# Spreading a second lane of work over a matmul stage, and re-dealing the buffers the two share

## The chip, the cores and the metric

The kernel runs on one core of one Trainium2 chip. The metric is the device time of one execution in microseconds; three runs gave 1947.91, 1949.51 and 1950.28 us, and the median, 1949.51 us, is the time before. One more execution was profiled; its numbers are in the section on the profile.

## The reference, cut to what matters

The model is one layer of a hybrid backbone on 256 latent and 256 context tokens of width 2048, all in float32. Its last part is an expert lookup ("PEER"): each token picks 8 x 16 = 128 of 16384 experts, and each expert has a row of 2048 numbers in a table u and one in a table v.

```python
def block(args):
    xb, eb, gb = args                       # tokens, their experts, their gates
    a = jnp.einsum('nd,nhkd->nhk', xb, jnp.take(u_tab, eb, axis=0))
    w = (gb * jax.nn.gelu(a.astype(jnp.float32))).astype(xb.dtype)
    return jnp.einsum('nhk,nhkd->nd', w, jnp.take(v_tab, eb, axis=0))
```

So per token there are 128 dot products with gathered u rows, a gelu, and a weighted sum of 128 gathered v rows. Each table has 16384 x 2048 x 4 bytes, 134 MB.

## The kernel before, in words

Everything up to row 0 of the u stage (projections, the mLSTM, the output projection, the queries) is not touched. The expert lookup splits the tokens in two groups.

- **The 192 dense tokens** (NA). For them TensorE multiplies the whole u table: 128 "rows" of the table (1 MB each, a transfer `...<-in_u_t` issued by SP), each in two halves. ScalarE makes `hi`, VectorE `lo` of each half (three buffers of each), and TensorE runs 16 pairs of matmuls `ups<-hf,hi` and `ups<-hf,lo` per row; ScalarE and VectorE then put the result in row i2 of the table W (`ut<-ups`, `W<-ut,ups`). This is the u stage. After it, `one_hots` and `pick` choose each token's 128 numbers out of W, four tokens at a time, and give weights `wA`; then one gather per token brings its 128 v rows (1 MB, `...<-in_v_rows`, issued by GpSimd, POOL in the profile) and eight matmuls `y<-...,wA` (`add_rows`) sum them. That is the y stage, 192 gathers long.
- **The 64 gathered tokens** are never multiplied with the whole table. For them a lane of work runs beside the u stage (`gen_gather`): 128 steps, each with a 1 MB gather. 64 are "u" steps (a gather of u rows, and on VectorE a dot product `...<-...,hB` of 2048 elements), 64 are "v" steps (a gather of v rows, eight matmuls into `adaps` or `yb`, and before each a small selector `wB` on ScalarE). The v steps follow the u steps by eight (`SUB`).

The kernel is written down in one pass by Python, with no scheduler behind it: instructions stand on each engine in the order in which the program issues them. The order comes from a planner's clock, `clock["t"]`, that each matmul moves on by an assumed duration. A lane is a generator that yields how long it wants to wait on that clock; after each half row `pump` advances the lanes that are due. In the lane of the gathered tokens each step ends with `yield GP`, 4.65 us of that clock; a lane that is behind may catch up by at most LAG, 3 us. What the lane hasn't done when the last row has been issued is issued by `drain()`, between the first `pick` and the y stage.

The gathers take their buffers from a list, `gaths`: `gath0`, `gath1` (and from row 66 `gath2`), and "lent" ones. W has 192 x 128 numbers per partition, 12 pieces of 8 KB; piece i is not written before row i*2048/192, so until then it can be lent. Pieces 1, 2, 3, 5, 7 and 9 are lent to the u table's transfers (`LENT_U`), 4, 6, 8 and, from row 66, 11 to gathers (`LENT`), and 10 from row 66 to u. Beside lent pieces, u has `rawA`, `rawB` and from row 66 `raw0`. `no_extra` ends the lending of a piece six rows ahead of its row; `lent_back` advances the lane, two rows ahead, until the piece is free. When the last row is out, `rawA`, `rawB`, `raw0` and `hB` become gather buffers too, so that the y stage rotates seven: the three `gath` and these four.

`gather` takes the first free buffer or returns False; `fetch` issues as many gathers of the list `to_get` as there are buffers. At the middle of the second half of the v steps the 192 dense gathers are put behind the others in `to_get`.

In the lines below L354 is the one place that issues a matmul, L133 the one that issues ScalarE and VectorE work, L268 the u table's transfer, L1367 the gather; so work is told apart by its tiles.

Of the kernel before, what the change touches and what calls it, by code (L numbers as in the profile page):

```python
# [34 lines left out]
KD = D // P  # L35
# [5 lines left out]
NK = 128  # L41
# [3 lines left out]
NA = T - NB  # L45
BT = 32
REP = P // BT
STEPS = PH * TOPK // REP
# [30 lines left out]
UTB = 3  # L79
RT_AT = 66  # L80
RT_DELAY = 60.0
GP = 4.65
NAF = 2
GY = 8.0
GATES_AT = 7
# [93 lines left out]
def build(tc, a, stack, dbg=None):  # L179
    nc = tc.nc  # L180
    ten, pool, sync = nc.tensor, nc.gpsimd, nc.sync
    clock = dict(t=0.0)
# [3 lines left out]
    def open_pool(name, side="left", **kw):  # L186
        cm = tc.tile_pool(name=name, bufs=1, side=side, reuse_waits="tile", **kw)
        return cm, cm.__enter__()

    def close_pool(p):  # L190
        p[0].__exit__(None, None, None)
# [10 lines left out]
    def mm_ps(name="mm"):  # L202
        return psp.tile([P, 512], F32, name=name, tag="mm", bufs=4)
# [30 lines left out]
    wides = Slots(lambda u: u.wide.used or u.wide.lo is not None, 2048)  # L234
# [101 lines left out]
    def drain(only=None):  # L336
        def left():
            return [k for k, q in lanes.items() if q and (only is None or k in only)]
        while left():
            for k in left():  # L340
                advance(k)
# [39 lines left out]
    def rstd_of(out, ss, n):  # L381
        vec.tensor_scalar(out, ss, 1.0 / n, EPS, op0=OP.mult, op1=OP.add)
        act.activation(out, out, AF.Sqrt)
        vec.reciprocal(out, out)
# [645 lines left out]
    R = {}  # L1030
    gaths = Slots(lambda u: u.used, 2048)

    LENT_U = (1, 2, 3, 5, 7, 9)
    LENT = (4, 6, 8, 11)
    x1d = tc.dram_tile([P, KD, T], F32, name="x1_spill")

    def make_hf(u):
        drain(only=("ada",))
        x1 = Y["x"]
        ss = mm_ps("ss1")  # L1040
        mm(ss[:, 0:T], ones, Y["sq"], start=True, stop=False)
        mm(ss[:, 0:T], ones, Y["last"], start=False, stop=True)
        prepare()
        rs = con.tile([P, T], F32, name="rs1", tag="rs1")
        rstd_of(rs, ss[:, 0:T], D)
        araws.drop(V["B"])
        close_pool(V["pb"])
        R["rh"] = open_pool("rh", side="right")
        R["rsb"] = open_pool("rsb", side="right")
        R["rs"] = open_pool("rs", side="right")  # L1050
        H, S, SB = R["rh"][1], R["rs"][1], R["rsb"][1]
        hf = H.tile([P, KD, 2, T], F32R, name="hf", tag="hf")
        hB = H.tile([P, D], F32, name="hB", tag="hB")
        R.update(hB=hB, hf=hf, hfs=hf.rearrange("p k s t -> p s k t"))
        R["keys"] = S.tile([P, 2, NK], F32, name="keys")
        sync.dma_start(R["keys"], a["keys"])
        sync.dma_start(x1d, x1)
        dump("x1", x1)
        n2 = 2 * PH * TOPK
        R["val"] = SB.tile([P, 2, n2], F32, name="val")  # L1060
        R["ix"] = SB.tile([P, 2, n2], U32, name="ix")
        R["sc"] = SB.tile([P, PH, TOPK], F32, name="sc")
        R["ci"] = SB.tile([P, PH, TOPK], U32, name="ci")
        R["e12"] = SB.tile([P, 3, PH, TOPK], F32, name="e12")
        R["h64"] = S.tile([P, KD, NB], F32, name="h64")
        shift, hm = mod[:, 3, 0], {}

        def scaled(k):
            hm[k] = S.tile([P, T], F32, name="hm1", tag="hm1", bufs=4)
            vec.scalar_tensor_tensor(hm[k], x1[:, k], gm[:, 2, k:k + 1], rs, op0=OP.mult, op1=OP.mult)  # L1070

        skew(KD, scaled,
             lambda k: act.activation(hf[:, k, 0], hm[k], AF.Identity, bias=shift[:, k:k + 1]),
             lambda k: vec.scalar_tensor_tensor(hf[:, k, 1], hm[k], shift[:, k:k + 1],
                                                hf[:, k, 0].bitcast(F32), op0=OP.add, op1=OP.subtract))
        spawn("hA", copy_hB())

        close_pool(pa)
        R["w"] = open_pool("w")
        R["W"] = R["w"][1].tile([P, NK, NA], F32, name="W")  # L1080
        flat = R["W"].rearrange("p e n -> p (e n)")
        room = [flat[:, c * 2048:(c + 1) * 2048] for c in range(NK * NA // 2048)]
        R["room"], R["scr"] = room, room[11]
        R["s0"] = room[10].rearrange("p (h k) -> p h k", k=NK)
        for i in LENT_U:
            wides.place(("row", i), room[i], i * 2048 // NA - 3)
        for i in LENT[:-1]:
            gaths.place(("lent", i), room[i])

    hBd = tc.dram_tile([P, D], F32, name="hB_spill")  # L1090

# [203 lines left out]
    def open_w(u):  # L1295
        drain(only=("hA", "score", "look"))
        close_pool(R["rs"])
        R["t"] = open_pool("wt")
        R["gp"] = open_pool("gp")
        gaths.add(R["gp"][1], "gath", F32, 2)  # L1300
        spawn("score", gen_route(1, RP1))
        spawn("score", gen_wait(RT_DELAY))
        spawn("score", gen_top(0, RP0))
        spawn("score", gen_route(0, RP0))

    def gen_wait(us):
        yield us
# [14 lines left out]
    def open_px(u):  # L1322

        drain(only=("score",))
        iT = R["iT"]
        vec.scalar_tensor_tensor(R["eA"], iT[:, 0, 0:NA], float(NK), iT[:, 1, 0:NA], op0=OP.mult, op1=OP.add)
        close_pool(R["rsb"])
        R["px"] = open_pool("px", side="right")
        wides.add(R["px"][1], "raw", F32, 1)
        gaths.add(R["px"][1], "gath", F32, 1)  # L1330

        wides.place(("row", 10), R["room"][10], 10 * 2048 // NA - 3)
        gaths.place(("lent", 11), R["room"][11])

    for i, tag in enumerate(("rawA", "rawB")):
        wides.take_over(pipe, tag, lambda i=i: all(s[3] is None or raws.done(s[3]) for s in raws.slots[2 * i:2 * i + 2]))
# [22 lines left out]

    got = collections.deque()  # L1360

    def gather(tab, idx):
        g = Unit(None, False, None)
        g.raw = gaths.take(g)
        if g.raw is None:
            return False
        pool.indirect_dma_start(out=g.raw, out_offset=None, in_=tab,  # L1367
                                in_offset=bass.IndirectOffsetOnAxis(ap=idx, axis=0))
        got.append(g)
        return True  # L1370

    to_get = collections.deque()
# [14 lines left out]
    def gen_gather():  # L1387

        aB, n = R["aB"], STEPS
        ops = []  # L1390
        for b in range(2):
            for s in range(n):
                ops += [("u", b, s)] + [("v", b, s - SUB)] * (s >= SUB)
                if s % SUB == SUB - 1:
                    ops.append(("fin", b, s + 1 - SUB))
            ops += [("v", b, s) for s in range(n - SUB, n)]

        ops.insert(ops.index(("v", 0, n - SUB)) + 2, ("hB", 1, 0))
        for kind, b, s in ops:
            if kind in ("u", "v"):  # L1400
                to_get.append((a[kind + "_rows"], R["idx"][:, b, s:s + 1]))
        scaled = {}

        def scale(b, s):
            w = scaled[b, s] = R["t"][1].tile([P, BT], F32, name="wB", tag="wB", bufs=2)
            act.activation(w, selb, AF.Copy, scale=aB[:, b, s:s + 1])

        fetch()
        yield 4.0
        for j, (kind, b, s) in enumerate(ops):  # L1410
            if kind == "v" and b == 1 and s == n // 2:
                to_get.extend((a["v_rows"], R["eA"][:, t:t + 1]) for t in range(NA))
            if kind == "fin":
                while "gates" not in R:
                    yield 1.0
                some = slice(s, s + SUB)
                act.activation(aB[:, b, some], aB[:, b, some], GELU)
                vec.tensor_tensor(aB[:, b, some], aB[:, b, some], R["gB"][:, b, some], op=OP.mult)
                if s == 0:
                    YB[b] = ada_ps() if b == 0 else sm_ps("yb")  # L1420
                yield 2.0
                scale(b, s)
                yield 0.0
                continue
            if kind == "hB":
                R["hB"] = R["rh"][1].tile([P, D], F32, name="hB", tag="hB")
                sync.dma_start(R["hB"], hBd)
                continue
            fetch()
            g = got.popleft()  # L1430
            if kind == "u":
                vec.scalar_tensor_tensor(g.raw, g.raw, 1.0, R["hB"], op0=OP.mult, op1=OP.mult,
                                         accum_out=aB[:, b, s:s + 1])
                g.used = True
            else:
                add_rows(YB[b], scaled.pop((b, s)), g, s == 0, s == n - 1)
                if (s + 1) % SUB:
                    scale(b, s + 1)
            fetch()
            yield GP  # L1440

    for i2 in range(NK):
        for i in LENT:
            row = i * 2048 // NA
# [308 lines left out]
```

## Time and profile before

| of the profiled execution | |
|---|---|
| its time | 1945.05 us |
| its span, first to last instruction | 1943.3 us |
| median of three runs without the profiler | 1949.51 us |
| PE busy / DVE / ACT / POOL, share of the span | 88% / 63% / 36% / 20% |
| moved by DMA | 670.20 MB, mean 345 GB/s |
| u stage: first and last `ups` matmul | 750.0 and 1424.8 us |
| y stage: first and last `y` matmul | 1448.7 and 1932.2 us |

PE is TensorE, PEld its weight loads, DVE VectorE, ACT ScalarE, POOL GpSimd, SP the engine that issues plain transfers. A busy share is an average over stages with different limits: PE is busy for 299.67 of the 300 us from 800 to 1100, and for 335.88 of the 480 us from 1440 to 1920. "Share" of DMA is the mean busy share of the 16 DMA engines. A wait is put down to what ended it. Program lines of the kernel after are four to five higher than those of the kernel before.

### The profile page before, as it was taken

The numbers are of one execution on the slowest core, as the hardware profiler recorded it, in microseconds if no ns is written. First come the engines' busy times: TensorE is split into PE (matmuls) and PEld (weight loads), VectorE is DVE, ScalarE is ACT, GpSimd is POOL, SyncE is SP. The second block draws the span as 40 slices with busy tenths as digits, with TensorE's granted clock in tenths as the row PEclk, the third lists the DMA queues.
The fourth block names the chain that finished last, engine by engine and source line by source line (L and its number), as shares of the span: only waits on it lengthen the run. The fifth ranks groups of instructions, "written<-read, shape, count | busy, mean of one in ns | idle before, by whom it ended". The sixth has DMA issues, their size and how long they took to land.

```text
span 1943.3 us, 29970 instructions
## 1 busy us (share of the span) xinstructions
PE 1713.3 (88%) x11882; PEld 1354.1 (70%) x11882; DVE 1226.5 (63%) x2498; ACT 702.1 (36%) x1105; POOL 384.2 (20%) x324
## 2 busy tenths in 40 slices
PE   4999999999899999899999999999976767667775
PEld 2689789979799899898988799889842222222221
DVE  5346868776698669889998587777633323323232
ACT  4235325555544544454444445444411100101000
POOL 0000000000000000332223232333333343333331
PEclk8999999999999899999999999999989888998888
DMA  9975878776688754999999999999989999999996
GB/s 396 393 266 178 291 239 303 274 249 213 212 321 308 274 185 147 390 413 371 390 384 407 395 403 417 378 389 400 389 349 420 420 421 421 421 420 421 421 421 287
DMA packets 115869, 670.20 MB, mean 345 GB/s; under 512 B 12688, under 2 KB 15248, under 8 KB 53264
## 3 DMA queue, kind: packets, MB, share of 16 engines
q1 hardware_dynamic: 69648, 332.72, 46.0%
q0 software_dynamic: 46080, 335.56, 42.2%
q8 instruction: 93, 1.52, 0.3%
q14 instruction: 48, 0.39, 0.1%
HBM read 662.99 MB, written 5.24 MB: 344 GB/s over the span
## 4 chain that ended last, share of the span: by engine, by line
PE 68%; DMA 23%; DVE 4%; issue 3%; ACT 1%; POOL 0%; SPq 0%; POOLq 0%; ACTq 0%; DVEq 0%
PE ups L354 29%; PE mm L354 25%; DMA gath<-in_v_rows,iT 8%; DMA hB<-in_v_rows,iT 5%; DMA raw<-in_v_rows,iT 3%; PE adaps L354 3%; PE y L354 2%; DMA rawB<-in_v_rows,iT 2%; DMA ring<-in_ada 2%; DMA rawA<-in_v_rows,iT 2%; PE pick L354 1%; PE num L354 1%; PE yb L354 1%; PE sm L354 1%; PE pc L354 1%
## 5 line engine op out<-in xcount | busy, mean ns | idle before, releaser
L354 PE MATMUL ups<-hf,hi 128*128 128x384 f32 x2048 | 601.5, 366 | 0.0
L354 PE MATMUL ups<-hf,lo 128*128 128x192 f32 x2048 | 515.6, 252 | 8.7 <-DVE lo L133 8.4
L354 PEld LDWEIGHTS ups<-hf,hi 128*128 128x128 f32 x2048 | 386.9, 189 | 48.5 <-issue 42.8
L354 PEld LDWEIGHTS ups<-hf,lo 128*128 128x128 f32 x2048 | 393.6, 192 | 12.2 <-DVE lo L133 12.2
L133 DVE SCALAR_TENSOR_TENSOR oh<-c,iT,pick 128x128 f32<-128x128 f32 x192 | 55.4, 345 | 305.4 <-PE pick L354 305.4
L133 DVE TENSOR_TENSOR lo<-rawA,hi 128x1024 fp32r<-128x1024 f32 x134 | 163.7, 1223 | 103.7 <-ACT hi L133 95.4
L133 DVE TENSOR_TENSOR lo<-rawB,hi 128x1024 fp32r<-128x1024 f32 x132 | 161.3, 1222 | 92.3 <-ACT hi L133 88.4
L1367 POOL DMA_INDIRECT W<-in_u_rows,iT x24 | 37.7, 1570 | 847.0 <-DMA W<-in_u_t 778.4
L133 ACT ACTIVATE hi<-rawA 128x1024 fp32r<-128x1024 f32 x134 | 141.6, 1057 | 147.8 <-PE ups L354 73.8
L1367 POOL DMA_INDIRECT gath<-in_v_rows,iT x119 | 135.1, 1136 | 270.6 <-PE y L354 119.0
L133 ACT ACTIVATE hi<-rawB 128x1024 fp32r<-128x1024 f32 x132 | 139.4, 1057 | 130.3 <-PE ups L354 64.6
L354 PE MATMUL mm<-xL,hi 128*128 128x256 f32 x864 | 181.1, 290 | 4.8 <-ACT xL L133 1.7
L133 ACT ACTIVATE hi<-W 128x1024 fp32r<-128x1024 f32 x114 | 120.8, 1060 | 149.7 <-PE ups L354 146.7
L133 DVE TENSOR_TENSOR lo<-W,hi 128x1024 fp32r<-128x1024 f32 x114 | 138.7, 1221 | 42.5 <-ACT hi L133 37.4
L354 PEld LDWEIGHTS mm<-xL,hi 128*128 128x128 f32 x864 | 144.0, 192 | 14.2 <-issue 7.5
L354 PE MATMUL y<-gath,wA 128*32 128x512 f32 x664 | 96.7, 660 | 64.2 <-DMA gath<-in_v_rows,iT 61.5
L133 DVE SCALAR_TENSOR_TENSOR adacc<-araw,early,adacc 128x1024 f32<-128x1024 f32 x120 | 152.4, 1278 | 0.0
L133 ACT ACTIVATE uA<-uA 128x4 f32<-128x4 f32 x48 | 9.9, 205 | 383.9 <-DVE oh L133 383.9
L354 PE MATMUL mm<-xL,lo 128*128 128x256 f32 x432 | 122.4, 283 | 0.0
L354 PEld LDWEIGHTS pick<-W,oh 128*128 128x128 f32 x384 | 77.8, 241 | 55.5 <-issue 52.7
L354 PE MATMUL mm<-hf,hi 128*128 128x256 f32 x512 | 98.7, 292 | 6.1 <-ACT hf L133 5.3
L354 PEld LDWEIGHTS y<-gath,wA 128*32 128x32 f32 x664 | 13.8, 111 | 121.0 <-DMA gath<-in_v_rows,iT 107.9
(284 smaller groups left out, 3021.6 us busy)
## 6 DMA issues: line engine op xcount, KB each, us to landing
araw<-in_ada SPq DMA_DIRECT2D x128, 512.0 KB
W<-in_u_t SPq DMA_DIRECT2D x57, 1024.0 KB
ring<-in_ada SPq DMA_DIRECT2D x32, 1024.0 KB
rawB<-in_u_t SPq DMA_DIRECT2D x28, 1024.0 KB
rawA<-in_u_t SPq DMA_DIRECT2D x28, 1024.0 KB
raw<-in_u_t SPq DMA_DIRECT2D x15, 1024.0 KB
rawB<-in_wout SPq DMA_DIRECT2D x16, 512.0 KB
rawA<-in_wout SPq DMA_DIRECT2D x16, 512.0 KB
```

The source lines that it names most:

```text
L133: return f(*args, **kw)
L354: ten.matmul(out, lhsT, rhs, start=start, stop=stop, skip_group_check=True, **kw)
L1367: pool.indirect_dma_start(out=g.raw, out_offset=None, in_=tab, in_offset=bass.IndirectOffsetOnAxis(ap=idx, axis=0))
```

## The change

The lane's wait is no longer a constant. When the u stage opens, the program works out when it will end on the planner's clock (`u_end`, 0.97 of the assumed matmul time of 128 rows and 64 v steps), and each step waits for the time that is left, divided by the steps that are left. Piece 9 goes from u to the gathers, and piece 10 too: u keeps five lent pieces (1, 2, 3, 5, 7), gathers have six (4, 6, 8, 9, then 10 and 11 from row 66). Dense gathers carry a row number that keeps them out of lent pieces.

```diff
-GP = 4.65
+LANE = 0.97
...
-    LENT_U = (1, 2, 3, 5, 7, 9)
-    LENT = (4, 6, 8, 11)
+    LENT_U = (1, 2, 3, 5, 7)
+    LENT = (4, 6, 8, 9, 10, 11)
...
-        for i in LENT[:-1]:
-            gaths.place(("lent", i), room[i])
+        for i in LENT[:-2]:
+            gaths.place(("lent", i), room[i], NK)
...
     def open_w(u):
...
+        R["u_end"] = clock["t"] + LANE * (NK * KD * (2 * NA / 2400.0 + 0.107) + 2 * STEPS * 4 * 0.244)
...
-        wides.place(("row", 10), R["room"][10], 10 * 2048 // NA - 3)
-        gaths.place(("lent", 11), R["room"][11])
+        for i in LENT[-2:]:
+            gaths.place(("lent", i), R["room"][i], NK)
...
-    def gather(tab, idx):
+    def gather(tab, idx, dense=False):
         g = Unit(None, False, None)
+
+        g.row = NK + 1 if dense else 0
...
-                to_get.extend((a["v_rows"], R["eA"][:, t:t + 1]) for t in range(NA))
+                to_get.extend((a["v_rows"], R["eA"][:, t:t + 1], True) for t in range(NA))
...
-            yield GP
+
+            yield max(0.5, (R["u_end"] - clock["t"]) / (len(ops) - j))
```

The instructions are the same in kind and number; their places and buffers differ. Counted in the programs' order, at the start of a row of the u stage, these steps of the lane have been issued, these gathers, and these rows of the u table:

| row | steps before, now | gathers before, now | u transfers before, now |
|---|---|---|---|
| 8 | 3, 3 | 8, 9 | 16, 15 |
| 66 | 60, 68 | 63, 72 | 73, 71 |
| 96 | 89, 100 | 93, 105 | 101, 100 |
| 122 | 116, 127 | 119, 130 | 126, 126 |

On ScalarE (ACT) at the end of the u stage: `ut` closes a row, `hi` is half a row of the u table, `wB` is the selector of a v step, `uA` and `ysb` belong to the y stage. Before:

```order
L133 ACTIVATE ut<-ups 128x192
L133 ACTIVATE hi_13974<-rawA 128x1024
L133 ACTIVATE iT<-iT 128x8
L133 ACTIVATE ut<-ups 128x192
L133 ACTIVATE wB<-c_68,iT 128x32 x3
L133 ACTIVATE ut<-ups 128x192
L133 ACTIVATE uA<-uA 128x4
L133 ACTIVATE wB<-c_68,iT 128x32 x5
```

And now:

```order
L133 ACTIVATE ut<-ups 128x192
L133 ACTIVATE hi_13997<-rawA 128x1024
L133 ACTIVATE hi_14017<-raw_13911 128x1024
L133 ACTIVATE ut<-ups 128x192
L133 ACTIVATE hi_14041<-raw_13911 128x1024
L133 ACTIVATE ut<-ups 128x192 x2
L133 ACTIVATE uA<-uA 128x4 x2
L133 ACTIVATE ysb<-adaps 128x512
```

Eight selectors stood here, three before the last row is closed and five behind it; now there is none, and the last v step stands at row 122.

On TensorE (PE) right behind the last `ups` matmul and the one-hots (`i`): `pick` reads W for four tokens, `yb` is a v step, `y` a dense token. Before:

```order
L354 MATMUL pick<-W,oh 128x128 x4
L354 MATMUL yb<-gath_13948,wB 32x512 x4
L354 MATMUL yb<-gath_14024,wB 32x512 x4
L354 MATMUL yb<-gath_14048,wB 32x512 x4
L354 MATMUL yb<-rawA,wB 32x512 x4
L354 MATMUL yb<-rawB,wB 32x512 x4
L354 MATMUL yb<-raw_14090,wB 32x512 x4
L354 MATMUL pick<-W,oh 128x128 x4
```

And now, from the pick on (two picks stand together, as x8, then four pairs of the one-hots of the third batch, of which the last is shown):

```order
L354 LDWEIGHTS ib
L354 MATMUL i_14158<-ib 128x128
L354 MATMUL y<-gath_13775,wA 32x512 x4
L354 MATMUL y<-gath_13807,wA 32x512 x4
L1592 MATMUL yT<-c_68,ysb 128x128 x4
L354 MATMUL y<-gath_13859,wA 32x512 x4
L354 MATMUL y<-rawA,wA 32x512 x4
L354 MATMUL ss_14203<-z,ones 128x32
```

Six v steps stood between the first pick and the first `y`; now none does, and the first three dense tokens lie in `gath` buffers, which were gathered into before the end of the u stage.

On SP, the u table's transfers a little behind row 66, in the buffers' names. Before:

```order
L268 DMA raw_11143<-in_u_t 128x2048
L268 DMA W<-in_u_t 128x2048 x2
L268 DMA rawB<-in_u_t 128x2048
L268 DMA rawA<-in_u_t 128x2048
L268 DMA raw_11384<-in_u_t 128x2048
```

And now:

```order
L268 DMA W<-in_u_t 128x2048
L268 DMA raw_10938<-in_u_t 128x2048
L268 DMA rawB<-in_u_t 128x2048
L268 DMA rawA<-in_u_t 128x2048
L268 DMA raw_11113<-in_u_t 128x2048
```

Before, u rotated five buffers here (two of them lent, W), down to three from its transfer 102 on; now it has `rawB`, `rawA` and `raw` alone from transfer 70 on.

## Rows read from the trace of the kernel before

**Rows 1.** Stages: busy us (instructions) per engine, granted clock, DMA share, GB/s.

```profile
core 0: us, PE busy (x) PEld busy (x) DVE busy (x) ACT busy (x) POOL busy (x), PEclk, DMA share, GB/s
800.00:860.00 60.00, 60.00 (x420) 56.99 (x420) 52.61 (x59) 31.56 (x44) 19.89 (x12) 1.00 1.01 420
800.00:1100.00 300.00, 299.67 (x2078) 270.12 (x2078) 264.28 (x497) 143.57 (x208) 87.36 (x56) 1.00 0.98 394
1100.00:1400.00 300.00, 297.39 (x2052) 270.24 (x2051) 220.34 (x243) 143.66 (x206) 94.36 (x57) 0.99 0.99 397
1412.00:1432.00 20.00, 18.62 (x131) 13.23 (x130) 8.56 (x24) 4.69 (x13) 8.24 (x8) 1.00 0.70 245
1440.00:1920.00 480.00, 335.88 (x2122) 129.87 (x2122) 153.27 (x706) 38.23 (x84) 178.36 (x189) 0.88 1.01 421
```

**Rows 2.** Waits on ScalarE in the u stage, 800 to 1425: us, times, longest.

```profile
ACT hi L133 <- PE ups L354: 296.3, 219, 3.3
...
ACT hi L133 <- DMA rawB<-in_u_t: 2.6, 1, 2.6
```

**Rows 3.** The chain that ended last: start us, us, what.

```profile
1125.06 50.62 PE ups L354 x352
...
1383.48 9.34 PE ups L354 x64
1393.82 9.34 PE ups L354 x64
...
1915.69 15.52 DMA gath<-in_v_rows,iT
```

**Rows 4.** The tile ups: ns min/median/max, first and last start.

```profile
L354 PE MATMUL ups<-hf,lo x2048: 249/250/529, 750.3 to 1424.8; 128*128 128x192 f32 x187
```

**Rows 5.** TensorE in order of time, 1418 to 1462: start us, us, tiles [idle before].

```profile
1424.94 1.07 PE L354 MATMUL yb<-gath,wB 128*32 128x512 f32 x8
...
1429.11 1.06 PE L354 MATMUL yb<-gath,wB 128*32 128x512 f32 x8
...
1438.05 1.93 PE L354 MATMUL yb<-gath,wB 128*32 128x512 f32 x8 [6.10 <-DMA gath<-in_v_rows,iT]
...
1445.52 1.07 PE L354 MATMUL yb<-raw,wB 128*32 128x512 f32 x8 [0.79 <-DMA raw<-in_v_rows,iT]
...
1448.67 1.06 PE L354 MATMUL y<-hB,wA 128*32 128x512 f32 x8
```

**Rows 6.** GpSimd, gathers: the lane's first, and around the end of the u stage.

```profile
778.81 2.11 POOL L1367 DMA_INDIRECT W<-in_u_rows,iT  x1 [778.36 <-DMA W<-in_u_t]
...
1414.81 1.78 POOL L1367 DMA_INDIRECT gath<-in_v_rows,iT  x1 [1.75 <-PE yb L354]
1422.85 0.94 POOL L1367 DMA_INDIRECT gath<-in_v_rows,iT  x1 [6.27 <-PE yb L354]
...
1431.29 0.94 POOL L1367 DMA_INDIRECT hB<-in_v_rows,iT  x1 [0.30 <-issue]
...
1450.04 0.94 POOL L1367 DMA_INDIRECT hB<-in_v_rows,iT  x1 [2.22 <-PE y L354]
```

**Rows 7.** VectorE: the lane's first dot product, and the first weights wA.

```profile
787.31 2.29 DVE L133 SCALAR_TENSOR_TENSOR W<-W,hB 128x2048 f32<-128x2048 f32 x1 [3.42 <-DMA W<-in_u_rows,iT]
...
1430.85 0.68 DVE L133 TENSOR_SCALAR wA<-c,uA 128x32 f32<-128x32 f32 x4
```

**Rows 8.** Two stretches of 2 us, columns as in Rows 1.

```profile
1422.00:1424.00 2.00, 2.00 (x19) 1.52 (x11) 0.00 (x0) 0.32 (x1) 0.94 (x1) 1.00 0.03 8
1424.00:1426.00 2.00, 2.00 (x17) 1.00 (x16) 0.35 (x1) 0.33 (x1) 0.00 (x0) 1.00 0.71 180
```

**Rows 9.** DMA queues, 800 to 860: packets, MB, share of 16 engines.

```profile
q0 software_dynamic: 1739, 12.67, 51.0%
q1 hardware_dynamic: 1709, 12.45, 49.9%
```

**Rows 10.** Page, costliest groups: ScalarE's hi and VectorE's lo, mean ns.

```profile
L133 DVE TENSOR_TENSOR lo<-rawA,hi 128x1024 fp32r<-128x1024 f32 x134 | 163.7, 1223 | 103.7 <-ACT hi L133 95.4
...
L133 ACT ACTIVATE hi<-rawA 128x1024 fp32r<-128x1024 f32 x134 | 141.6, 1057 | 147.8 <-PE ups L354 73.8
```

## The prediction

> **What bounds the kernel now.** I read the stages first [rows 1]. In the u stage two things are nearly full at once: TensorE is busy for 299.67 of 300 us and 297.39 of 300 us, and the DMA engines show a share of 0.98 and 0.99. Busy alone doesn't say which of the two holds, so next come the waits. ScalarE's `hi` waits 296.3 us for TensorE to give a buffer back and, the longest of its transfer waits, 2.6 us for one from DRAM [rows 2]. Data is there before TensorE wants it: TensorE bounds the u stage, DMA only keeps step. From 1440 to 1920 it is the other way round: DMA share 1.01 at 421 GB/s, TensorE busy for 70% [rows 1]. The last gather is issued at 1915.69 and has landed 15.52 us later, at 1931.2, and the chain runs through it [rows 3]; the rest of the span, 12.1 us, is the last tokens' end.
>
> Between the two stages DMA runs dry: from 1412 to 1432 it moves 245 GB/s [rows 1], so 20 x (1 - 245/421) = 8.4 us of its time are lost. The reason stands in the rows of TensorE and GpSimd: the last `ups` matmul starts at 1424.8 [rows 4], but seven v steps come behind it, from 1424.94 to 1446.6 [rows 5], and their gathers are issued one by one as buffers come free, 1414.81, 1422.85 and on [rows 6]. The first gather for a dense token goes out only at 1431.29 (into hB) and is used at 1448.67 [rows 5, 6]. So the y stage, which is a pure stream of 192 gathers, starts its stream late. Its pace: first landing 1448.67, last 1931.2, 191 gathers between, 482.5/191 = 2.526 us each [rows 3, 5].
>
> **The change part by part.**
>
> *The seven v steps move into the u stage.* There they cost TensorE time, since TensorE is the bound. Without v steps 352 `ups` take 50.62 us, 0.1438 us each, and 64 of them (two rows) 9.20 us; with one v step the same two rows repeat after 1393.82 - 1383.48 = 10.34 us [rows 3]. A v step costs 1.14 us. 57 are inside the u stage now, 64 will be: 7 x 1.14 = 8.0 us, so it would end at 1424.8 + 8.0 = 1432.8, if nothing else in it moves.
>
> *More gathers in the first half.* By row 66 the lane has issued 72 gathers instead of 63, and u 71 transfers instead of 73: 7 MiB more (each is 1 MiB) in the stretch that is 800 to 1100 now. There DMA moved 394 GB/s x 300 us = 118.2 MB, 112.7 MiB [rows 1]; it will be 119.7. With both queues full it moved 420 GB/s from 800 to 860 [rows 1], 2.497 us per MiB, so this needs 299 us; TensorE will take 300 + 4 v steps x 1.14 = 304.6 us. It fits at 98%, and the gathers have a cushion: four to six are issued ahead, at 4.7 us a step (304.6 us for the 65 steps from row 8 to 66) some 19 us or more, where one alone took 8.5 us beside u transfers (issued 778.81, used 787.31) [rows 6, 7]. At 98% some land late all the same, and a late one holds VectorE or TensorE, whose queues run in order: behind a waiting dot product stand the `lo` that TensorE needs next. The least is nothing; the most, with DMA at 394 GB/s, is 119.7 x 1.0486/0.394 - 304.6 = 14 us. I take 3 us, near the lower end, since the 420 was measured with the same two streams. VectorE itself has room: 264.28 of 300 us now [rows 1], plus four dot products of 2.29 us [rows 7], 273 of 305. In the second half there is less to add (rows 66 to 122: 58 gathers instead of 56, 55 u transfers instead of 53), and I put nothing there. So the u stage ends at X = 1432.8 + 3 = 1435.8.
>
> *The buffers.* Pieces 9 and 10 taken from u shorten its lead; price nothing as long as three buffers do, which is a rival below. For the gathers they make the cushion just used. The dense gathers, kept out of lent pieces, get gath0 to gath2 before the end: three, which land under the last rows, as the v steps end at row 122. Then rawA, rawB, raw and hB as u gives them back, about at rows 125 to 127; those four land by about X + 2, since only 2 u transfers run beside them.
>
> *The start of the y stage.* TensorE now goes from the first pick straight on. Its first weights `wA` are ready at 1430.85 + 0.68 = 1431.5 [rows 7], 6.7 us behind the last `ups`; that chain (one-hots, pick, VectorE, gelu) is unchanged, so the first `y` runs at X + 6.7 and ends 1.06 us later [rows 5]. Seven gathers are in, 128 to 134 counted over all 320; number 135 reuses the first buffer. Now hB was issued at 1450.04, 0.3 us behind the end of the `y` that freed it (1448.67 + 1.06) [rows 5, 6], so 135 is issued at X + 8.1. DMA has been dry for some 5 us by then; the 2 MiB that SP fetches for the residual fill that hole, which they don't today. From issue to landing on an idle DMA no row shows it: below is the bare transfer of 2.5 us, above the 8.5 us of the shared one. Nearest is the issue at 1422.85, behind which DMA goes from 8 GB/s to 180 between 1424 and 1426 [rows 6, 8]: about 1.6 us to the first bytes, and 2.5 us for the rest, 4.1 us. I take that. (The Trainium skill, "DMA: Bandwidth & Descriptors", on the anatomy of one DMA of the gpsimd path, gives 2.0 us plus the bytes at 436 GB/s, so 4.4 us here as an estimate, and the sum would be 0.3 us later.) So 135 lands at X + 12.2 and DMA is full from there, as TensorE is busy for only 0.70 of the time that DMA takes for a token [rows 1].
>
> *The sum.* Number 319, the last, is 184 gathers later: X + 12.2 + 184 x 2.526 = X + 477.0 = 1912.8, against 1931.2: 18.4 us less. With the same end the profiled execution would go from 1945.05 to 1926.7 us. The three runs have their median 4.5 us above the profiled one; the difference carried over, 1949.51 - 18.4 = 1931 us.
>
> **The rivals.**
>
> *DMA in the u stage does no more than it does now.* If 394 and 397 GB/s are the mixture's ceiling and not the demand, the first half takes 14 us longer than TensorE; the second, 300 x 397 = 119.1 MB today plus 4 MiB, takes 123.3/0.397 = 311 against some 302, 9 us more. Together 23 in the place of my 3: X is 20 us later and the gain of 18 is gone, 1951 us, no change. For it speaks the share of 0.98 already, against it 420 GB/s with q0 and q1 at 51.0% and 49.9% and TensorE 60.00 of 60 us busy [rows 1, 9].
>
> *Three buffers starve u; this ends slower.* From transfer 70 on u has three. A buffer is taken up again every three rows, 15.5 us (a row is 10.34/2 = 5.17 us [rows 3]); behind the landing a `hi` of 1.06 us and two `lo` of 1.22 us take 3.5 us of that [rows 10], so a transfer may need 12.0 us, and each us beyond costs 0.33 us a row on the 52 rows to 122: 17 us. It decides from 13.1 us, where the whole gain is lost. One us more, 14.1, gives 1949.5 + 17 = 1967 us. If the engines served requests in proportion to their number, three u transfers among six or seven gathers would get a third of 420 GB/s, 7.5 us each, and two behind each other 15. Against it stand the u table's transfers from 102 on as they are today: three buffers too, and ScalarE's longest wait for a transfer is 2.6 us [rows 2]. And from 800 to 860 u, with eight buffers against five, got 49.9%, not 62% [rows 9]: half, so 5 us a transfer, 10 us for two. Without these two rows I would give this rival 0.25. (The Trainium skill, the same page, on queues, rings and completion order, says that each DMA engine goes round robin between the queues with work. By that rule u keeps its half however many gathers wait; the trace agrees, 49.9%.)
>
> *The steps don't get done in time*, and the v steps still stand behind the last row: then nothing changes, 1949 us. The order of the instructions excludes it, the last v step stands at row 122.
>
> **How the numbers follow.** A measurement tells 0.2%, 4 us, from no change. My forecast, 18 us with a reach of 8 (5 us more stall, 4 us more latency) to 28 (the stalls at the u stage's start shrink too), gets 0.72, all of it faster. The DMA ceiling gets 0.18: it is a matter of degree, 0.06 faster, 0.09 same, 0.03 slower. Three buffers get 0.10: 0.02 same, 0.08 slower. So faster 0.78, same 0.11, slower 0.11. The forecast's own range is 1921 to 1942; to hold 8 in 10 with the ceiling's upper part it reaches to 1949.
>
> **What would show it.** No `yb` behind the last `ups`; the last `ups` at 1430 to 1440; the first `y` 6 to 8 us behind it, not waiting for a transfer; GB/s from 800 to 1100 above 405 with TensorE still full; the first gather for a dense token some 25 us ahead of the last `ups`; 2.5 us a gather to the end. Wrong it would be if TensorE or VectorE waits for gathers in the first half (the ceiling), if `hi` waits for `in_u_t` from row 70 on (three buffers), or if the last `ups` comes later than 1453.

## The result, and the profile after

The changed kernel takes 1932.93 us (median of 4 runs, 1929.97 to 1934.56), the kernel before 1948.71 us in the same comparison (4 runs): ratio 0.9923, 95% interval 0.991 to 0.9936. A second comparison gave 1931.18 against 1947.82 us, 0.9918 (0.9901 to 0.9934). The forecast was 1931 us. By the medians the gain is 15.8 and 16.6 us. The profiled execution took 1929.97 us with a span of 1928.2 us, 15.1 us less than the 1943.3 before; 18.4 had been worked out. Of all the runs below one, of nine buffers the second time, took 2520.52 us at a mean granted clock of 0.676, against 0.942 to 0.960 in the others, and its row leaves it out.

The stages first, with the columns of [rows 1]:

```profile
800.00:1100.00 300.00, 300.00 (x2089) 267.92 (x2089) 264.51 (x496) 142.79 (x210) 94.22 (x62) 1.00 1.01 415
1100.00:1400.00 300.00, 294.48 (x2038) 264.21 (x2038) 218.47 (x242) 141.64 (x209) 92.11 (x59) 0.99 0.99 404
1412.00:1432.00 20.00, 20.00 (x142) 20.00 (x141) 10.39 (x13) 8.40 (x11) 4.41 (x4) 1.00 0.69 257
1440.00:1920.00 480.00, 338.25 (x2121) 130.54 (x2114) 152.44 (x699) 38.19 (x83) 173.95 (x185) 0.86 0.99 410
1480.00:1900.00 420.00, 296.96 (x1854) 115.97 (x1858) 129.65 (x610) 28.54 (x66) 155.88 (x166) 0.86 1.01 421
```

From 800 to 1100 DMA moves 415 GB/s, where it was 394, and TensorE is busy for all of the 300 us. So 394 was what the old pace asked for, not what the engines can do. From 1412 to 1432 DMA still runs dry, 257 GB/s. The 410 GB/s from 1440 to 1920, against 421 before, don't mean a slower y stage: the last gather lands at 1916.7 now, inside that stretch, and from 1480 to 1900 the stage has its 421. What is less full is its start, which comes with the experiments.

The tile `ups` (ns min/median/max, first and last start) answers to [rows 4]:

```profile
L354 PE MATMUL ups<-hf,lo x2048: 249/250/529, 750.3 to 1432.8; 128*128 128x192 f32 x187
```

The last `ups` starts 8.0 us later, and that is what the seven v steps were to cost. From here on it is best to split the span at that start. Before: 1424.8 us up to it and 1943.3 - 1424.8 = 518.5 us behind it. After: 1432.8 and 495.4. The change pays 8.0 us in the u stage and gets 23.1 us behind it.

TensorE around the end of the u stage (start us, us, tiles, idle before), against [rows 5]:

```profile
1406.61 1.06 PE L354 MATMUL yb<-gath,wB 128*32 128x512 f32 x8
...
1438.52 1.92 PE L354 MATMUL y<-gath,wA 128*32 128x512 f32 x16
1440.75 0.66 PE L1592 MATMUL yT<-c,ysb 128*128 128x128 f32 x4 [0.30 <-ACT ysb L133]
...
1442.22 1.04 PE L354 MATMUL y<-rawA,wA 128*32 128x512 f32 x8
1445.82 0.41 PE L354 MATMUL ss<-z,ones 128*128 128x32 f32 x2 [2.56 <-DVE z L133]
1446.06 1.98 PE L354 MATMUL pick<-W,oh 128*128 128x128 f32 x8
...
1448.40 1.94 PE L354 MATMUL y<-rawB,wA 128*32 128x512 f32 x8
...
1461.16 0.41 PE L354 MATMUL ss<-z,ones 128*128 128x32 f32 x2 [3.34 <-DVE z L133]
```

The last v step is at 1406.61, 26 us ahead of the last `ups`; behind it stands none. The first `y` comes 5.7 us behind the last `ups`, a little sooner than the 6 to 8 us expected, and waits for no transfer. What had not been reckoned with stands between the first tokens: the closing work of the two gathered blocks (`yT`, `ss`), and `ss` waits 2.56 and 3.34 us for VectorE's `z`, with the next tokens' `y` queued behind it. Before, the same block work stood there too. The wait costs a second time: TensorE is busy for 0.44 of the 3 us from 1443 to 1446, its granted clock then falls to 0.50 (1.2 GHz) from 1448 to 1451, and the `y` of `rawB` takes 1.94 us there, where that of `rawA` took 1.04.

GpSimd's gathers, against [rows 6]:

```profile
1398.76 1.78 POOL L1371 DMA_INDIRECT gath<-in_v_rows,iT  x1 [3.98 <-PE yb L354]
1402.22 1.78 POOL L1371 DMA_INDIRECT gath<-in_v_rows,iT  x1 [1.68 <-PE yb L354]
1407.97 1.77 POOL L1371 DMA_INDIRECT gath<-in_v_rows,iT  x1 [3.98 <-PE yb L354]
1424.14 0.94 POOL L1371 DMA_INDIRECT rawA<-in_v_rows,iT  x1 [14.39 <-DVE lo L133]
...
1439.89 0.94 POOL L1371 DMA_INDIRECT gath<-in_v_rows,iT  x1 [8.50 <-PE y L354]
...
1443.94 0.94 POOL L1371 DMA_INDIRECT rawA<-in_v_rows,iT  x1 [0.30 <-issue]
1450.64 0.94 POOL L1371 DMA_INDIRECT rawB<-in_v_rows,iT  x1 [5.77 <-PE y L354]
```

Three gathers for dense tokens go out 34 to 25 us ahead of the last `ups`, then nothing for 14.39 us, since all buffers are taken. Number 135 goes out at 1439.89, as soon as the first `y` has given its buffer back. After 1443.94 the next waits 5.77 us for `y`: that `y` is the one held by `ss` above.

The last gather of the chain, against the last of [rows 3] (start us, us):

```profile
1901.17 15.49 DMA gath<-in_v_rows,iT
```

It lands at 1916.7, 14.5 us earlier than before, and 11.5 us are left to the end.

ScalarE's waits from 800 to 1425 (us, times, longest), against [rows 2]:

```profile
ACT hi L133 <- PE ups L354: 262.1, 198, 2.5
...
ACT hi L133 <- DMA rawA<-in_u_t: 12.1, 6, 3.0
ACT hi L133 <- DMA rawB<-in_u_t: 11.5, 6, 3.0
ACT hi L133 <- DMA raw<-in_u_t: 10.5, 5, 2.8
```

With fewer buffers `hi` now waits for u transfers 17 times, 34.1 us in all, and 16 of these waits lie behind 1100, where u has three buffers. So the sign that the prediction named for too few buffers did show. But nothing of it reaches TensorE:

```profile
1140.00:1400.00 260.00, 260.00 (x1812) 229.97 (x1811) 183.35 (x199) 122.81 (x183) 79.33 (x50) 1.00 0.99 403
```

The lead of u has become shorter and is still enough.

### The profile page after: what moved, and what is told of

The parts are those of the page before. It is cut to its first block, busy times and chain, and to the rows that moved or that the text cites. A ratio compares the mean times of both kernels' runs of the same rounds, so it can differ in the third digit from the quotient of the medians.

```text
span 1928.2 us, 29971 instructions
## 1 busy us (share of the span) xinstructions
PE 1710.3 (89%) x11882; PEld 1354.9 (70%) x11882; DVE 1226.9 (64%) x2498; ACT 701.6 (36%) x1105; POOL 382.9 (20%) x324
## 4 chain that ended last, share of the span: by engine, by line
PE 69%; DMA 21%; issue 4%; DVE 4%; ACT 1%; POOL 1%; SPq 0%; POOLq 0%; ACTq 0%; DVEq 0%
PE ups L354 29%; PE mm L354 25%; DMA gath<-in_v_rows,iT 6%; DMA raw<-in_v_rows,iT 6%; DMA hB<-in_v_rows,iT 4%; PE adaps L354 3%; PE y L354 2%; PE yb L354 2%; DMA ring<-in_ada 2%; DMA rawB<-in_v_rows,iT 2%; PE num L354 1%; PE sm L354 1%; PE pick L354 1%; DMA rawA<-in_v_rows,iT 1%; DVE lo L133 1%
## 5 line engine op out<-in xcount | busy, mean ns | idle before, releaser
L133 DVE TENSOR_TENSOR lo<-rawA,hi 128x1024 fp32r<-128x1024 f32 x148 | 180.7, 1222 | 114.2 <-ACT hi L133 107.2
L133 DVE TENSOR_TENSOR lo<-rawB,hi 128x1024 fp32r<-128x1024 f32 x146 | 178.3, 1222 | 105.4 <-ACT hi L133 93.1
L1371 POOL DMA_INDIRECT W<-in_u_rows,iT x34 | 51.5, 1514 | 889.2 <-DMA W<-in_u_t 778.3
L133 ACT ACTIVATE hi<-rawA 128x1024 fp32r<-128x1024 f32 x148 | 156.3, 1056 | 155.8 <-PE ups L354 67.8
L133 ACT ACTIVATE hi<-rawB 128x1024 fp32r<-128x1024 f32 x146 | 154.3, 1057 | 154.4 <-PE ups L354 78.1
L1371 POOL DMA_INDIRECT gath<-in_v_rows,iT x115 | 130.2, 1132 | 251.5 <-PE y L354 128.8
L354 PE MATMUL y<-gath,wA 128*32 128x512 f32 x672 | 106.3, 720 | 52.6 <-DMA gath<-in_v_rows,iT 52.6
L133 ACT ACTIVATE hi<-W 128x1024 fp32r<-128x1024 f32 x76 | 80.5, 1060 | 103.4 <-PE ups L354 98.1
L133 DVE TENSOR_TENSOR lo<-W,hi 128x1024 fp32r<-128x1024 f32 x76 | 92.4, 1220 | 16.3 <-ACT hi L133 14.4
L354 PE MATMUL pick<-W,oh 128*128 128x128 f32 x384 | 97.1, 410 | 1.1 <-issue 1.1
## 6 DMA issues: line engine op xcount, KB each, us to landing
ring<-in_ada SPq DMA_DIRECT2D x32, 1024.0 KB, 12.1
```

What stands on the lines that cost most here:

```text
L133: return f(*args, **kw)
L354: ten.matmul(out, lhsT, rhs, start=start, stop=stop, skip_group_check=True, **kw)
```

## The experiments

In the table the columns "to last ups" (from the first `ups` to the last) and "behind it" (to the end of the span) come from the profile of each kernel, time and ratio from its runs. The first `ups` starts between 750.1 and 755.5 us, another time in each profile though nothing ahead of it differs; that shift is as large as some of the effects, and the two columns are free of it.

| kernel | to last ups | behind it | median us | ratio to before, 95% |
|---|---|---|---|---|
| before | 674.5 | 518.5 | 1948.71 | |
| changed | 682.5 | 495.4 | 1932.93 | 0.9923 (0.991 to 0.9936) |
| changed, again | 682.8 | 495.6 | 1931.18 | 0.9918 (0.9901 to 0.9934) |
| pace alone | 682.7 | 496.6 | 1933.22 | 0.9926 (0.9913 to 0.9938) |
| buffers alone | 675.6 | 519.8 | 1949.95 | 1.0016 (1.0006 to 1.0026) |
| four steps left behind | 676.3 | 510.9 | 1941.87 | 0.9977 (0.9966 to 0.9987) |
| two buffers for u | 726.7 | 497.5 | 1980.73 | 1.0153 (1.0121 to 1.0185) |
| closing work later | 683.2 | 491.8 | 1930.35 | 0.9905 (0.9889 to 0.9922) |
| nine buffers | 682.6 | 491.1 | 1928.25 | 0.9901 (0.9885 to 0.9918) |
| nine buffers, again | 682.7 | 491.1 | 1930.74 | 0.9918 (0.9901 to 0.9935) |
| both | 682.6 | 493.2 | 1928.24 | 0.9897 (0.9881 to 0.9914) |

**The pace alone.** The changed kernel with the old deal of buffers.

```
-    LENT_U = (1, 2, 3, 5, 7)
-    LENT = (4, 6, 8, 9, 10, 11)
+    LENT_U = (1, 2, 3, 5, 7, 9)
+    LENT = (4, 6, 8, 11)
...
-        for i in LENT[:-2]:
+        for i in LENT[:-1]:
...
-        for i in LENT[-2:]:
+        wides.place(("row", 10), R["room"][10], 10 * 2048 // NA - 3)
+        for i in LENT[-1:]:
```

> The new pace with the old buffers: u has pieces 1, 2, 3, 5, 7, 9 and later 10, the gathers 4, 6, 8 and later 11; the steps stand at the same rows as in the changed kernel (the last v step at row 122), with one gather less ahead (71 issued at row 66, not 72; 104 at row 96, not 105). Theory A, the gain is the v steps taken from behind the u stage, and the buffers are incidental: the same time as the changed kernel, 1931 to 1935 us, last ups matmul at 1432 to 1434 us in the profile. Rival B, the pace needs the two pieces for the gathers, since DMA is at its ceiling in the first half: gathers land late and hold VectorE, the last ups matmul comes 5 us or more later, 1938 to 1946 us.

Measured: 1933.22 us, within 0.3 us of the changed kernel. Its stage, columns as in [rows 1]:

```profile
800.00:1100.00 300.00, 300.00 (x2090) 267.91 (x2090) 264.55 (x497) 141.92 (x209) 93.17 (x61) 1.00 1.01 414
```

Same traffic, same busy TensorE. The last `ups` starts at 1436.1, not at 1432 to 1434, but the first one also starts 3.1 us later in this profile. By the two columns the pace alone pays 8.2 us and gets 21.9, where the whole change pays 8.0 and gets 23.1. So the pace carries all of the gain but about 1 us, which the times don't show; the new deal of buffers is not needed for the rest.

**The buffers alone.** The changed kernel with the old pace.

```
-            yield max(0.5, (R["u_end"] - clock["t"]) / (len(ops) - j))
+            yield 4.65
```

> The new buffers with the old pace of 4.65 us: steps at the rows of the kernel before, seven v steps behind the last row, 60 of them issued at row 66. Theory A: no gain, 1946 to 1951 us, last ups at 1425, last dense landing at 1931. Rival B, part of the gain comes from the buffers (gathers further ahead): a third of the gain or more, 1944 us or less.

```profile
800.00:1100.00 300.00, 298.44 (x2063) 270.82 (x2062) 263.21 (x497) 143.14 (x207) 81.14 (x55) 1.00 0.98 392
```

Measured: 1949.95 us, DMA at 392 GB/s, 519.8 us behind the last `ups`. More buffers for gathers don't raise the traffic while the steps themselves come no earlier. Alone they even lose a little: 1.1 us up to the last `ups` and 1.3 behind it, and the interval of the ratio lies just above 1. With these two runs both halves of the change stand apart, but they don't simply add: 13.7 us gained and 2.4 lost make 11.3, where the whole change has 15.1. Why the buffers lose beside the old pace and not beside the new one was not followed.

**Four steps left behind.** `LANE` stretches the plan so that v steps 124 to 127 stand behind the last row.

```
-LANE = 0.97
+LANE = 1.03
```

> The changed kernel with LANE 1.03 in the place of 0.97: four v steps (124 to 127) stand behind the last row instead of none. Theory A: the gain shrinks with the steps behind, 15.8 x 3/7 = 7 us are left, 1940 to 1944 us; last ups at 1428, first dense gather issued behind it. Rival, the gain comes from the fuller DMA in the u stage and not from what stands behind it: 1931 to 1936 us, since 124 of 128 steps are still in the u stage.

Measured: 1941.87 us. Of TensorE's `yb` from 1400 on (ns min/median/max, first and last start) the last now stands behind the last `ups`, which starts at 1426.4:

```profile
L354 PE MATMUL yb<-gath,wB x64: 592/617/1062, 1405.9 to 1440.1; 128*32 128x512 f32 x64
```

Three of the seven steps are moved, and the gain is 6.1 us against 15.8 for seven: 2.0 and 2.3 us a step. The gain goes with the number of steps behind the last row, as the theory has it. One of its numbers is off: the last `ups` was expected at 1428, and the u stage pays 1.8 us for the three steps instead of 3.4. TensorE's wait for `e` at row 66 is 1.0 us shorter here than before; the other 0.6 were not followed.

**Two buffers for u.** The third buffer, which u gets at row 66, is left out.

```
-        wides.add(R["px"][1], "raw", F32, 1)
```

> The changed kernel, but raw0 is not given to u: from transfer 70 on u has two buffers, rawA and rawB. The size of the rival about starving u: a row then takes (landing time + 3.5)/2 us; with a landing of 8 us that is 5.75 us a row against 5.17, 0.6 us on some 57 rows, 33 us: 1960 to 1970 us, with ScalarE's hi waiting for in_u_t in nearly every row. If the lead of u has slack to spare, two buffers do as well: 1931 to 1936 us.

Measured: 1980.73 us, all of the loss ahead of the last `ups` (726.7 against 682.5). ScalarE's waits from 1100 to 1490 and one stretch of this kernel:

```profile
ACT hi L133 <- DMA rawB<-in_u_t: 91.4, 23, 8.4
ACT hi L133 <- DMA rawA<-in_u_t: 76.1, 26, 8.3
```

```profile
1100.00:1400.00 300.00, 273.37 (x1791) 242.94 (x1790) 199.29 (x221) 122.31 (x181) 66.46 (x52) 0.95 0.91 356
```

So the rival of the starving u stage is a real mechanism, and three buffers are enough where two are not. `hi` waits for u 49 times in some 58 rows, as expected, but the price was set too low: 1960 to 1970 us was expected, and 44 us are lost in the u stage. DMA itself is idle for part of the stretch now (share 0.91), so it isn't short of bandwidth but of a buffer to write to. The trace shows which part of the formula was off. From one issue to the next into the same buffer 12.2 us pass on the mean (28 turns of each buffer): 7.6 until the transfer has landed, 4.3 from the first `hi` to the end of the second `lo`, and 0.3 between the two. The formula had 8 and 3.5. The landing was priced well; the split takes longer than the bare sum of its three instructions.

**Closing work later.** The changed kernel, in which the blocks' closing work may first be stepped behind group 4 of the y stage.

```
-            some()
+            if j >= 4:
+                some()
```

> The changed kernel, in which the closing work of the blocks (yT, ss, the final norm) may first be stepped behind group 4 of the y stage instead of behind its first token. Theory: in the changed kernel the closing work of the two gathered blocks stands between the first dense tokens on TensorE and waits there (2.56 and 3.34 us for VectorE's z); that holds tokens and so buffers, and DMA is not full before about 1460 us. Out of the way, gathers 136 to 145 come in 22.7 us instead of 25.2: the end 2 to 4 us earlier, 1929 to 1931 us, ratio to the kernel before 0.990 to 0.992; PE has no wait for z between 1438 and 1465. Rival (the start is held by the number of buffers, or by the first landing alone): 1932 to 1935 us, ratio 0.992 to 0.993, while the waits for z are gone all the same.

Two stretches of 20 us of the changed kernel, and then of this one (its last `ups` is 5.8 us later, 1438.6):

```profile
1440.00:1460.00 20.00, 14.95 (x105) 6.87 (x98) 12.13 (x43) 5.58 (x10) 9.65 (x10) 0.91 0.97 359
1460.00:1480.00 20.00, 15.12 (x98) 5.93 (x98) 8.07 (x33) 3.27 (x6) 7.49 (x8) 0.91 1.02 423
```

```profile
1440.00:1460.00 20.00, 17.53 (x127) 9.39 (x127) 10.79 (x57) 0.82 (x4) 9.38 (x10) 1.00 1.00 405
1460.00:1480.00 20.00, 13.08 (x92) 5.39 (x92) 5.31 (x28) 0.90 (x3) 6.65 (x8) 1.00 1.01 421
```

No `ss` stands between the first tokens any more, between 1425 and 1480 TensorE waits for transfers and for nothing of VectorE's, and the stretch behind the last `ups` falls from 495.4 to 491.8 us. (From 1445.8 to 1465.8, as far behind its last `ups` as 1440 to 1460 is in the changed kernel, DMA moves 399 GB/s.) That is the 2 to 4 us expected. Its time, 1930.35 us, is 2.6 us below the changed kernel, with intervals that overlap: the profile shows the gain, the timed runs don't establish it.

**Nine buffers.** Of the room in which the residual lands it fills two quarters; the other two go to gathers.

```
-    O["x"] = R["rh"][1].tile([P, KD, T], F32, name="x2", tag="hf")
+    x2 = R["rh"][1].tile([P, 4, 2048], F32, name="x2", tag="hf")
+    O["x"] = x2[:, 0:2].rearrange("p a (k t) -> p (a k) t", t=T)
+    for i in (2, 3):
+        gaths.place(("x2", i), x2[:, i])
```

> The changed kernel with two more gather buffers from the moment the score tile's room is free (nine instead of seven in the y stage). Theory: behind the last row the queue runs dry (4 GB/s in 1420 to 1424 us in the changed kernel) since every buffer holds a gather that waits for the first y; two more gathers can go out before it, so 2 x 2.5 = up to 5 us: 1928 to 1931 us, ratio 0.989 to 0.991, with two more dense gathers issued ahead of the first y. Rival (the score tile's room comes free too late, or the tail's pace alone counts): 1932 to 1935 us, ratio 0.992 to 0.993.

> The changed kernel with nine gather buffers in the y stage, a second time. Theory (the two more gathers fill the dry stretch behind the last row, 3.7 us by the first profile): 1926 to 1931 us, 3 to 4 us below the changed kernel of the same call. Rival (the gap of 4.7 us between the medians was chance): no more than 1 us between the two.

> The changed kernel as it is, a second time, to be compared in one call with the one with nine buffers. If its time repeats: 1930 to 1935 us, ratio to the kernel before 0.991 to 0.994.

GpSimd in the second run of it, and one stretch (its last `ups` is at 1433.4):

```profile
1433.88 0.94 POOL L1371 DMA_INDIRECT x<-in_v_rows,iT  x1 [1.95 <-PE i L354]
1435.12 0.94 POOL L1371 DMA_INDIRECT x<-in_v_rows,iT  x1 [0.30 <-issue]
1440.43 0.94 POOL L1371 DMA_INDIRECT gath<-in_v_rows,iT  x1 [4.37 <-PE y L354]
```

```profile
1440.00:1460.00 20.00, 14.93 (x102) 7.25 (x98) 10.15 (x37) 4.81 (x8) 7.57 (x8) 0.83 1.00 420
```

The two extra gathers go out 6 us ahead of the first that waits for a `y`, the stretch from 1440 to 1460 is full (420 GB/s against 359), and 491.1 us are left behind the last `ups`, in both profiles, against 495.4 and 495.6 of the changed kernel in its two: 4.4 us. In time the two runs don't agree: 1928.25 us, 4.7 below the changed kernel, and then 1930.74 against 1931.18 (four runs from 1926.31 to 1931.39). By its own measure, no more than 1 us between the two, the second run speaks for the rival in time. So against the changed kernel the profiles show the gain and the times don't establish it, as the start of the u stage alone moves by as much; against the kernel before it is about 1%.

**Both.** Nine buffers and the closing work later.

> The changed kernel with both: the closing work from group 4 on, and nine gather buffers. If the two losses are separate they add: 4 to 9 us below the changed kernel, 1924 to 1929 us, ratio 0.987 to 0.990. If both only fill the same dry stretch behind the last row, it comes out as the better of the two alone.

Its stretch from 1440 to 1460:

```profile
1440.00:1460.00 20.00, 14.94 (x114) 5.98 (x112) 8.40 (x46) 0.62 (x3) 9.37 (x10) 0.99 1.01 423
```

Measured: 1928.24 us (1927.87 to 1929.33), 4.7 us below the changed kernel. That lies in the range for two losses that add, and it is also what nine buffers had alone, so the time doesn't tell the two cases apart. The profile does: 3.6 and 4.4 us added would leave 487.4 us behind the last `ups`, and 493.2 are left, 2.1 more than with nine buffers alone. Both fill the same gap in the stream of gathers, and once DMA is full from 1440 on (423 GB/s) nothing is left to fill there; where the 2.1 us come from was not followed. It has the lowest median here, though by no more than the scatter.

## Why the prediction was right, and which of its terms were off

Its sum in five terms, X being the start of the last `ups`:

| term | predicted | measured |
|---|---|---|
| X | 1435.8 | 1432.8 |
| gather 135 issued | X + 8.1 | X + 7.1 |
| until it has landed | 4.1 | 8.2 |
| 184 more gathers | 464.8 | 468.6 |
| from the last landing to the end | 12.1 | 11.5 |
| span | 1924.9 | 1928.2 |

*The mechanism* held: TensorE bounds the u stage, gathers the y stage, and the seven steps behind the last row held the second stream up. The experiments with the pace alone and with four steps left show it from both sides.

*The cost of the moved steps*, 7 x 1.14 = 8.0 us from [rows 3], was met to the tenth (1432.8 - 1424.8).

*The issue of gather 135* came 1.0 us sooner than worked out. The 6.7 us from the last `ups` to the first weights were read from the kernel before as unchanged; but there one of the seven v steps, 1.07 us at 1424.94 [rows 5], stands between the last `ups` and the one-hots, and it has moved too.

*The 3 us for late gathers* did not come; the lower bound of that term, nothing, was right. The number of `ups` (here of `lo`) by 1140 us is the same in both kernels, with the same start, first before, then after:

```profile
L354 PE MATMUL ups<-hf,lo x1156: 249/250/529, 750.3 to 1139.9; 128*128 128x192 f32 x193
```

```profile
L354 PE MATMUL ups<-hf,lo x1156: 249/250/529, 750.3 to 1139.8; 128*128 128x192 f32 x193
```

By then 32 v steps have run in both, and all of the additional gathers of the first half have. VectorE waits for no transfer from 800 to 1140 in either kernel. A single wait did become longer, TensorE's for VectorE's `e` at row 66, 2.6 us before and 5.5 after; two of the lane's dot products stand ahead of `e` now. By 1140 it had been made up: the changed kernel has its 32nd v step at 1083.8, the kernel before has four of the 32 behind row 66.

```profile
PE it L1278 <- DVE e L133: 5.5, 1, 5.5
```

*The ceiling of DMA*, the rival with most chance, falls with 415 GB/s. *Three buffers* fall with the transfers' time, which must stay under 12.0 us by the prediction. From 1150 to 1400, where u has its three, the queues (packets, MB, share) and the transfers of u (count, KB each, median us to landing) show:

```profile
q1 hardware_dynamic: 6872, 50.01, 49.7%
q0 software_dynamic: 6903, 50.28, 49.2%
...
rawA<-in_u_t SPq DMA_DIRECT2D x16, 1024.0 KB, 9.6
raw<-in_u_t SPq DMA_DIRECT2D x16, 1024.0 KB, 9.4
rawB<-in_u_t SPq DMA_DIRECT2D x15, 1024.0 KB, 9.6
```

The queue of u keeps its half, and 9.4 to 9.6 us a transfer are 2.4 below the bound; the prediction had worked out 10. (The Trainium skill, "DMA: Bandwidth & Descriptors", section "Queues, rings and completion order", says that each DMA engine goes round robin between the queues with work; 49.7 against 49.2% agrees.)

*The latency of gather 135* is the step that failed, and in two parts. The first is "the 2 MiB that SP fetches for the residual fill that hole". They don't. That fetch needs the room of `hf`, which the last `ups` reads, so it can only start behind it, while DMA's hole (4 GB/s from 1420 to 1424) lies ahead of it. Transfers issued from 1424 to 1440, three of them (count, KB each, us to landing), the third from 1439 to 1440 on:

```profile
x<-x_spill SPq DMA_DIRECT2D x1, 2048.0 KB, 10.2
rawA<-in_v_rows,iT POOLq DMA_INDIRECT x1, 5.5
...
gath<-in_v_rows,iT POOLq DMA_INDIRECT x1, 8.2
```

The queues from 1440 to 1446 (packets, MB, share), q1 that of the fetch and q0 that of the gathers:

```profile
q0 software_dynamic: 147, 1.10, 61.3%
q1 hardware_dynamic: 67, 0.84, 32.8%
```

The fetch, issued at 1433.10, lands at 1443.3, and until then gather 135, issued at 1439.89, shares the engines with it. (For the same reason `hB`, the last of the seven, lands at X + 7.7 and not by X + 2.) Behind the fetch the gathers are alone, and still slow: 287 to 328 GB/s in each us from 1443 to 1447, with about 3 MiB of them on the way, where 2 to 2.5 MiB are enough for 424 GB/s from 1448 to 1452. So the 8.2 us are the fetch's doing only in part; how large a part was not tried by moving it, and what slows the gathers behind it stays open.

The second part is the 4.1 us for an idle DMA. `rawA`, issued at 1424.14 into a DMA that had moved next to nothing for 4 us, took 5.5 us, with one more gather issued 1.24 us behind it; with the pace alone the same case took 5.4. The row that served as nearest could have told: by its 180 GB/s from 1424 to 1426 [rows 8] 0.36 of the 1.05 MB had come, and the rest takes at least 1.6 us more, 4.8 us in all. The prediction gave a lone gather the full rate from its first bytes on. (The Trainium skill, "DMA: Bandwidth & Descriptors", section "Anatomy of one DMA — SWDGE (gpsimd) path", fits 2.0 us plus the bytes at 436 GB/s, 4.4 us here as an estimate; the 5.5 and 5.4 us measured decide.)

*The pace.* 2.526 us was measured from the first `y` on a landed gather, 1448.67 [rows 5]; but TensorE had been at other work, and by the packets counted in the trace that gather had landed at about 1446.2. From there the pace is 485.0/191 = 2.539, which makes 184 x 0.013 = 2.4 of the 3.8 us. The other 1.4 lie at the start: DMA moves 311 GB/s from 1452 to 1456, behind the gather that had waited 5.77 us for the `y` held by `ss`. That both experiments there shorten the stretch by 3.6 and 4.4 us shows that the stream was not full at once, as the prediction took it to be.

The misses partly cancel: -3.0 for X, +6.9 from X to the last landing, -0.6 behind it; together the 3.3 us between 18.4 and 15.1. That the time came out within 2 us of the forecast is therefore in part luck: the 3 us for late gathers, which weren't needed, paid for nearly half of the 6.9 us that the way from X to the last landing was short.

## What to carry to other kernels

Where one resource bounds a stage and another the next, work of the second kind that is left over between them should be paced to end with the first stage; its price there is what it takes of the bounding engine, read from the spacing of the same rows with it and without. A mean GB/s below the known peak says nothing about a ceiling until the demand has been raised. And at a seam between two streams, list what else wants the same engines in just those microseconds, which room it waits for and what stands between the first items in the in-order queue: mean busy shares of the stage don't hold there.

## What the runs showed of the hardware that had not been expected

Two queues together kept 414 to 415 GB/s for 300 us beside a TensorE busy for all of it, so at this level the mixture costs DMA next to nothing against the 421 GB/s of the gathers alone. A gather of 1 MiB landed 5.4 to 5.5 us behind its issue into an idle DMA, after 8.2 at the seam, and after 15.9 in the median of the changed kernel's y stage. The issue of a gather took GpSimd 1.68 us in the median from 800 to 1410 (0.94 to 1.97), and 0.94 in the y stage; which neighbour makes the difference was not tried. And the first `ups` starts anywhere from 750.1 to 755.5 us in eleven profiles whose work ahead of it is the same, while the stretches behind it repeat to some tenths: a difference of a few us is better read from such a mark on than from the whole time.
